# Low parts of the opening weights, and the decay of the recurrent states, moved between engines in a two-layer decoder kernel

## The chip, the cores and the metric

The kernel runs on one core of a Trainium2 chip. The metric is the time of one execution in microseconds of the device. The profile and the trace come from one execution on that core.

## What is computed

One step of a small decoder runs for 520 tokens at once: a prompt of 512 tokens and 8 sample tokens with caches of their own. Layer 0 is sliding-window attention beside a state-space scan, layer 1 is a gated DeltaNet; a SwiGLU feed-forward net, ffn(0) and ffn(1), follows each. Cut to what matters here:

```python
def swiglu(h, w_gate, w_up, w_down):
    return (jax.nn.silu(h @ w_gate) * (h @ w_up)) @ w_down

# gated_delta_rule, one step of the scan; a sample token is one such step
u = u0_c - jnp.einsum('bhik,bhkv->bhiv', kcd_c, s)
s = s * gl_c[..., None, None] + jnp.einsum('bhjk,bhjv->bhkv', kdec_c, u)

# trunk, per layer
h = rmsnorm(x, norm_mix_pre[l])
m = ...                                  # the mixer: projections of h, then the scan
x = x + rmsnorm(m, norm_mix_post[l])
f = swiglu(rmsnorm(x, norm_ffn_pre[l]), w_ffn_gate[l], w_ffn_up[l], w_ffn_down[l])
x = x + rmsnorm(f, norm_ffn_post[l])
```

The model width is 1024, the hidden width of the feed-forward net 2816. In layer 1, 16 heads for each of 8 sample tokens have a state of 128 x 128 that is read, multiplied by a decay, added to and written back.

## The kernel before

**Matmuls.** Activations lie with features on the partitions and tokens along the row, in two halves: half 0 has 256 tokens, half 1 has 264. Weights and activations are split into a high part that TensorE takes and the rest, the low part. Each product is the sum of three matmuls: high weight by high activation, high weight by low activation, low weight by high activation (`lin`). In the profile `whi` and `wlo` are the two parts of a weight block, and `Hh`, `Hl`, `p`, `bm` and `X` hold the two parts of activations in different stages.

**Weights.** A raw load (`raw`, two buffers, issued by SyncE's queue) brings 256 columns, two tiles of 128. `split` works on a unit of 128 x 512, half a tile's weights: it writes the high part, on ScalarE or, for each `hi_v`-th unit, on VectorE, and the low part, raw minus high, at line 193: on GpSimd for each `lo_pool`-th unit and on VectorE otherwise; `lo_pool` 0 means VectorE always. There are four buffers each for `whi` and `wlo`. The stages set both numbers: in layer 1's projections every low part goes to GpSimd, in ffn(1) every third.

**Parked low parts.** While ffn(0) runs, `park` loads 40 units of later weights (staged in `cs`), computes their low parts ahead of time (staged in `b`) and writes them to DRAM tensors named `pk`. When `split` meets such a unit it makes only the high part and loads the low part by a DMA on SyncE's queue. `PTILES` lists the tiles: of layer 1's first projection tiles 10 to 15, 0 to 7 and 16 to 21, in which 16 to 21 are the first six of the sixteen value tiles.

**Openings.** A stage's projection can begin when the norm of the stage before is done, first for half 0, then for half 1. So `group` does the first three or four tiles for half 0 and then for half 1: in ffn(0) and ffn(1) two gate tiles and two up tiles, in layer 1 a small tile of 32 columns and tiles 8 and 9. Their weights are prepared during the out projection of the stage before; the last tiles take buffers of their own (`p`, `b`, `cs`), since the ring has four. `out_proj` ends with `lo_pool` set to 1, so the units of the next opening group have their low parts on GpSimd, at the time at which VectorE does the norm (`rs`, `R`, then the products with `R`, the sums into the residual, and `Hl`).

**Layer 1's middle.** After the key and query tiles VectorE does the triangular elimination (line 302, `p` and `b`, with transposes at lines 1502, 1530 and 1531), while TensorE goes on with the value tiles; each is evacuated by VectorE (`cs<-acc,R`), and its convolution is shared by VectorE (`cs<-cs,cw`), ScalarE and GpSimd (`cs<-cs,p`, `cs<-cs,ex`).

**States.** `state_steps` runs in ffn(1): 34 steps, of which the inner 32 do a state block of one sample token and four heads. Step n stores block n-2, decays block n-1 (on GpSimd, `cs<-cs,small`, 128 x 512) and adds to it twice (VectorE, `cs<-b,CS,cs`, 128 x 256), and loads block n and its addend (`b<-ud`). ffn(1) goes through its 22 gate and 22 up tiles in 11 pairs of two and two, and takes a step after each tile from the second pair on, 40 places in all. The Silu of the gate tiles and the high casts of the hidden tiles are on ScalarE.

**Order.** The program is built by a scheduler that simulates the engines and orders each engine's instructions from it; the order in the source is only its input, marks such as `issue_after` and `high_priority` steer it. A changed instruction can therefore move others all over the program. Every engine, and every queue of DMAs, takes its instructions in the order emitted.

Of the kernel before, what the change touches and what calls it, by code (L numbers as in the profile page):

```python
# [13 lines left out]
ALU = mybir.AluOpType  # L14
# [104 lines left out]
 'yd': 'G'}  # L119


PTILES = [*range(10, 16), *range(8), *range(16, 22)]


def KN(n, v, *others):
# [97 lines left out]
class Ker:  # L223
# [112 lines left out]
    def group(s, w, xh, xl, nkt):  # L336

        w = [list(v) for v in w]
        ps = [{} for _ in w]
        for t in range(len(w)):  # L340
            if t % 2 == 0:
                a = s.acc()
            ps[t][0] = a[:, 256 * (t % 2):256 * (t % 2) + 256]
        for t in range(len(w)):
            ps[t][1] = (s.acc() if t < 2 else s.mx())[:, 0:HW[1]]
        for h in (0, 1):
            for t, v in enumerate(w):
                s.lin(v, xh, xl, nkt, (h,), ps[t])
        return ps

    def lnexp(s, ins):
# [145 lines left out]
    def out_proj(s, rows, xh, xl, nkt, mp, n, l, pre, tail=2, final=False):  # L497

        s.mp, s.sqs = mp, ([], [])
        if not final:  # L500
            tail = KN("tail%d%d" % (n, l), tail, 2, 3, 4)

        def evac(ps, ot):
            ins = None
            with s.tc.high_priority():
                for h in ps:
                    if ot == 7:
                        s.sqs[h].append(s.tms(HW[h]))
                        ins = s.act(s.sqs[h][0], ps[h], AF.Square)
                    if ot == 7 and final and h:  # L510
                        s.ts(mp[:, ot, HALF[h]], ps[h], s.gain(n, l, ot))
                    else:
                        s.act(mp[:, ot, HALF[h]], ps[h], scale=s.gain(n, l, ot))
                    if ot < 7:
                        s.add_sq(h, ps[h], ot == 0, s.tmp)
            return ins

        for ot in range(8 - tail):
            evac(s.lin(rows(ot), xh, xl, nkt), ot)
            if final and ot == 2:  # L520
                s.final_early()
        s.lo_pool = KN("lp_t%d%d" % (n, l), 2, 1, 3, 4)
        for h in (0, 1):
            for ot in range(8 - tail, 8):
                ins = evac(s.lin(rows(ot), xh, xl, nkt, (h,)), ot)
            if h == 0:
                with s.tc.issue_after(ins):
                    s.nc.scalar.preload_act_table_set("natural_log_exp_and_others")
                if final:
                    s.final_first()  # L530
                else:
                    s.pre = pre()
                    s.prenorm(*s.pre, 0, s.residual(n == 3, 0))
        if final:
            s.final_last()
        s.lo_pool, s.hi_v = 1, 0

    def spill(s):
        s.xd = s.dr.tile([128, KD * NT], F32, tag="xd", name="xd", bufs=2)
# [547 lines left out]
    def ffn(s, l):  # L1087
# [4 lines left out]
        x = s.lay("Hh"), s.lay("Hl")  # L1092
# [17 lines left out]
        if l == 0:  # L1110
            w = s.i["w_gdn_in"][0]
            s.copy_every = 0
            s.W.todo = [(w, 128 * t, k0) for t in PTILES for k0 in (0, 4)]
        s.lo_pool = KN("lp_f%d" % l, 1, 2, 3)
        s.hi_v = KN("hv_f%d" % l, 0, 2, 3, 4, 1)
        if l:
# [4 lines left out]
        for p in range(11):  # L1121
            sg = {}
            for t in (2 * p, 2 * p + 1):
                ps = first[t] if p == 0 else s.lin(s.W.tile(g, 128 * t, kts), *x, 8, ps=spare(t < 2 + KN("ma_f%d" % l, 0, 1, 2)))
                for h in (0, 1):
                    sl = (s.B("cs", NT * (t % 2), NT) if l == 0 else sgs if t % 2 else s.accT)[:, HALF[h]]
                    gt = s.tmp(HW[h])
                    with s.tc.high_priority():
                        s.tt(gt, ps[h], s.R2[:, HALF[h]], ALU.mult)
                    with s.tc.issue_after(s.norm_ins):  # L1130
                        ins = s.act(sl, gt, AF.Silu)
                    sg[t, h] = sl
                if l == 0 and p:
                    s.W.park(ins)
                if l and p:
                    next(states, None)
            for t in (2 * p, 2 * p + 1):
                ps = first[2 + t] if 2 + t < len(first) else s.lin(s.W.tile(u, 128 * t, kts), *x, 8)
                for h in (0, 1):
                    gt = s.tmp(HW[h])  # L1140
                    with s.tc.high_priority():
                        s.tt(gt, sg[t, h], ps[h], ALU.mult)
                    a = hh(t, h)
                    ins = s.act(a, gt)
                    s.tt(hl(t, h), gt, a.bitcast(F32), ALU.subtract)
                if l == 0 and p:
                    s.W.park(ins)
                if l and p:
                    next(states, None)
        for _ in states if l else ():  # L1150
            pass
# [715 lines left out]
    def state_steps(s):  # L1867
# [4 lines left out]
        gb = s.small(8, 2, 16)  # L1872
# [5 lines left out]
        for n in range(4 * NS + 2):  # L1878
            with s.tc.issue_after(s.last_load):
                if n > 1:  # L1880
                    s.dma(state(o["sgs"], n - 2), S(n - 2))
                if 0 < n < 4 * NS + 1:
                    t, (b, h) = S(n - 1), at(n - 1)
                    s.tt(t, t, gb[:, b, 0, h].unsqueeze(2).to_broadcast([128, 4, 128]), ALU.mult, s.nc.gpsimd)
                    for j in range(2):
                        v = slice(2 * j, 2 * j + 2)
                        s.stt(t[:, v], ub(n - 1)[:, v], s.kqs[:, h.start // 2 + j, b, 0:1], t[:, v], ALU.mult, ALU.add)
# [53 lines left out]
```

## Time and profile before

| | us |
|---|---|
| median of 3 runs (1893.59 to 1896.18) | 1893.84 |
| the profiled execution | 1886.62 |
| its span, first to last instruction | 1884.8 |
| TensorE busy | 1744.3 |
| VectorE busy | 1160.9 |
| ScalarE busy | 769.3 |
| GpSimd busy | 890.8 |

The mean granted clock of TensorE is 0.966. In rows of the profile, PE is TensorE's matmul, PEld its weight load, DVE is VectorE, ACT ScalarE, POOL GpSimd and SP SyncE. A row of a group gives line, engine, operation, output and inputs, shapes and count; then busy time and the mean of one in ns; then the idle time of the engine ahead of it and who ended that. A row of the timeline gives start, duration, engine, line, operation, and in brackets the idle time just before with what ended it. A row of the chain gives start and duration of a piece.

### The profile page before, as it was taken

The numbers are of one execution on the slowest core, as the hardware profiler recorded it, in microseconds if no ns is written. First come the engines' busy times: TensorE is split into PE (matmuls) and PEld (weight loads), VectorE is DVE, ScalarE is ACT, GpSimd is POOL, SyncE is SP. The second block draws the span as 40 slices with busy tenths as digits, with TensorE's granted clock in tenths as the row PEclk, the third lists the DMA queues.
The fourth block names the chain that finished last, engine by engine and source line by source line (L and its number), as shares of the span: only waits on it lengthen the run. The fifth ranks groups of instructions, "written<-read, shape, count | busy, mean of one in ns | idle before, by whom it ended". The sixth has DMA issues, their size and how long they took to land.

```text
span 1884.8 us, 36666 instructions
## 1 busy us (share of the span) xinstructions
PE 1744.3 (93%) x14263; PEld 1656.7 (88%) x14263; DVE 1160.9 (62%) x2325; ACT 769.3 (41%) x1868; POOL 890.8 (47%) x793
## 2 busy tenths in 40 slices
PE   7889999898999999989977888989999999999996
PEld 6878777598999999978977887888998999999995
DVE  6898879539433331168799967788703866753025
ACT  5432235555433333346765655644435311111222
POOL 2565657234666663342342564544557333323452
PEclk9999999898999999999988999999999999999998
DMA  7336766354556553346753113246435588863554
GB/s 258 129 126 184 221 193 179 130 154 126 157 182 189 185 175 100 92 141 212 245 172 112 43 45 110 60 125 186 135 91 180 160 257 262 262 206 123 160 160 152
DMA packets 328784, 300.39 MB, mean 159 GB/s; under 512 B 14529, under 2 KB 299910, under 8 KB 327442
## 3 DMA queue, kind: packets, MB, share of 16 engines
q1 hardware_dynamic: 327958, 297.37, 50.7%
q8 instruction: 112, 1.84, 0.4%
q10 hardware_dynamic: 652, 0.68, 0.1%
q14 instruction: 62, 0.51, 0.1%
HBM read 261.98 MB, written 72.52 MB: 177 GB/s over the span
## 4 chain that ended last, share of the span: by engine, by line
PE 50%; DVE 18%; DMA 9%; ACT 4%; issue 4%; POOL 2%; SPq 1%; DVEq 0%; ACTq 0%; POOLq 0%
PE acc L296 43%; PE ma L296 4%; DVE p L302 3%; DVE cs L309 3%; PE mb L296 2%; DMA b<-ud 2%; DMA raw<-in_w_ffn_down_dram 1%; DVE wlo L193 1%; ACT L312 1%; DMA cs<-in_state_gdn_dram 1%; POOL cs L302 1%; SPq L324 1%; DVE b L302 1%; DVE Hl L309 1%; PE mb L299 1%
## 5 line engine op out<-in xcount | busy, mean ns | idle before, releaser
L193 POOL TENSOR_TENSOR wlo<-raw,whi 128x512 fp32r<-128x512 f32 (+2 forms) x342 | 453.2, 1328 | 504.9 <-ACT whi L317 304.3
L296 PE MATMUL acc<-Hl,whi 128*128 128x256 f32 (+1 forms) x2576 | 561.4, 291 | 29.7 <-DVE cs L302 18.1
L296 PEld LDWEIGHTS acc<-Hl,whi 128*128 128x128 f32 x2576 | 419.2, 193 | 43.8 <-issue 18.8
L317 ACT CAST whi<-raw 128x512 fp32r<-128x512 f32 (+3 forms) x392 | 234.3, 603 | 436.2 <-PE acc L296 335.5
L296 PE MATMUL acc<-Hh,whi 128*128 128x256 f32 (+1 forms) x1824 | 390.2, 289 | 9.6 <-DVE sq L302 6.3
L296 PE MATMUL acc<-Hh,wlo 128*128 128x256 f32 (+1 forms) x1824 | 389.7, 289 | 1.2 <-DVE wlo L193 1.2
L296 PEld LDWEIGHTS acc<-Hh,whi 128*128 128x128 f32 x1824 | 293.6, 192 | 17.2 <-DVE sq L302 9.2
L296 PEld LDWEIGHTS acc<-Hh,wlo 128*128 128x128 f32 x1824 | 293.4, 192 | 9.0 <-issue 6.7
L296 PE MATMUL acc<-bm,whi 128*128 128x256 f32 (+1 forms) x1136 | 234.8, 290 | 0.1
L296 PE MATMUL acc<-p,whi 128*128 128x264 f32 (+1 forms) x1280 | 226.4, 284 | 0.0
L193 DVE TENSOR_TENSOR wlo<-raw,whi 128x512 fp32r<-128x512 f32 (+1 forms) x141 | 117.6, 835 | 140.3 <-ACT whi L317 137.7
L296 PEld LDWEIGHTS acc<-p,whi 128*128 128x128 f32 x1280 | 187.8, 190 | 0.8 <-DVE p L302 0.5
L296 PEld LDWEIGHTS acc<-bm,whi 128*128 128x128 f32 x1136 | 181.1, 193 | 2.8 <-issue 2.1
L318 DVE CAST whi<-raw 128x512 fp32r<-128x512 f32 x131 | 65.4, 503 | 179.8 <-PE acc L296 136.4
L296 PE MATMUL acc<-Hl,wlo 128*128 128x256 f32 (+1 forms) x752 | 169.7, 295 | 1.2 <-DMA wlo<-pk 0.7
L296 PE MATMUL acc<-p,wlo 128*128 128x256 f32 (+1 forms) x704 | 162.0, 284 | 7.1 <-DVE wlo L193 7.1
L296 PEld LDWEIGHTS acc<-Hl,wlo 128*128 128x128 f32 x752 | 126.1, 196 | 3.9 <-issue 1.6
L296 PEld LDWEIGHTS acc<-p,wlo 128*128 128x128 f32 x704 | 117.4, 189 | 8.0 <-DVE wlo L193 7.9
L296 PE MATMUL acc<-X,whi 128*128 128x264 f32 (+1 forms) x512 | 99.1, 288 | 1.1 <-ACT X L312 1.1
L309 DVE SCALAR_TENSOR_TENSOR cs<-cs,cw 128x512 f32<-128x512 f32 x100 | 90.4, 905 | 12.0 <-POOL cs L302 7.0
L302 POOL TENSOR_TENSOR cs<-cs,small 128x512 f32<-128x512 f32 x48 | 55.1, 1152 | 87.8 <-DMA cs<-in_state_gdn_dram 68.8
L296 PEld LDWEIGHTS acc<-X,whi 128*128 128x128 f32 x512 | 79.3, 193 | 2.4 <-ACT X L312 2.2
(466 smaller groups left out, 2989.6 us busy)
## 6 DMA issues: line engine op xcount, KB each, us to landing
raw<-in_w_gdn_in_dram SPq DMA_DIRECT2D x24, 1024.0 KB
raw<-in_w_ffn_gate_dram SPq DMA_DIRECT2D x22, 1024.0 KB
raw<-in_w_ffn_up_dram SPq DMA_DIRECT2D x22, 1024.0 KB
raw<-in_w_ffn_down_dram SPq DMA_DIRECT2D x20, 1024.0 KB
raw<-in_w_hyb_in_dram SPq DMA_DIRECT2D x16, 1024.0 KB
out_sv_dram<-in_cache_attn_v_dram SPq DMA_DIRECT2D x16, 1023.0 KB
out_sk_dram<-in_cache_attn_k_dram SPq DMA_DIRECT2D x16, 1023.0 KB
cs<-in_w_gdn_in_dram SPq DMA_DIRECT2D x40, 256.0 KB
```

The source lines that it names most:

```text
L193: eng.tensor_tensor(out=lo[:, :nk, d:d + n], in0=raw[:, :, o:o + n], in1=hi[:, :nk, d:d + n].bitcast(F32), op=ALU.subtract)
L296: s.nc.tensor.matmul(out, lhsT=lhsT, rhs=rhs, start=start, stop=stop, skip_group_check=skip)
L299: s.nc.tensor.transpose(out, in_, s.ident[0:in_.shape[0], 0:in_.shape[0]])
L302: return (eng or s.nc.vector).tensor_tensor(out=out, in0=a, in1=b, op=op).ins
L309: return s.nc.vector.scalar_tensor_tensor(out=out, in0=a, scalar=sc, in1=b, op0=op0, op1=op1).ins
L312: return s.nc.scalar.activation(out=out, in_=in_, func=f, **kw).ins
L317: return s.nc.scalar.copy(out, in_).ins
L318: return (s.nc.vector if e == "V" else s.nc.gpsimd).tensor_copy(out, in_).ins
L324: return (eng or s.nc.sync).dma_start(out=out, in_=in_).ins
```

## The change

Five edits:

1. The 40 parked units are others: tiles 8 and 9 of layer 1, the second and third of its opening group, come in, and the eight units of ffn(1)'s opening group; value tiles 16 to 21 go out.
2. `out_proj` ends with `lo_pool` 0 in place of 1: opening units that are not parked have their low parts on VectorE. In ffn(0) these are all eight, in layer 1 the two small ones of the 32-column tile.
3. In `group` the second half goes by row tiles, all tiles at one row tile and then the next.
4. The states begin one pair of tiles later, so 36 places are left for the 34 steps.
5. The decay of a state block is four activations of 128 x 128 with a scale per partition on ScalarE, in place of one multiplication of 128 x 512 on GpSimd.

```diff
-PTILES = [*range(10, 16), *range(8), *range(16, 22)]
+PTILES = [*range(8, 16), *range(8)]
...
-        for h in (0, 1):
+        for t, v in enumerate(w):
+            s.lin(v, xh, xl, nkt, (0,), ps[t])
+        for n in range(nkt):
             for t, v in enumerate(w):
-                s.lin(v, xh, xl, nkt, (h,), ps[t])
+                kt, hi, lo = v[n]
+                for lhs, x, st, sp in ((hi, xh, n == 0, False), (hi, xl, False, False), (lo, xh, False, n == nkt - 1)):
+                    s.mm(ps[t][1], lhs, x(kt, 1), st, sp)
...
-        s.lo_pool, s.hi_v = 1, 0
+        s.lo_pool, s.hi_v = 0, 0
...
-            s.W.todo = [(w, 128 * t, k0) for t in PTILES for k0 in (0, 4)]
+            s.W.todo = ([(w, 128 * t, k0) for t in PTILES for k0 in (0, 4)] +
+                        [(s.i[n][1], 128 * t, k0) for n in ("w_ffn_gate", "w_ffn_up") for t in (0, 1) for k0 in (0, 4)])
...
-                if l and p:
+                if l and p > 1:
                     next(states, None)
...
-                    s.tt(t, t, gb[:, b, 0, h].unsqueeze(2).to_broadcast([128, 4, 128]), ALU.mult, s.nc.gpsimd)
+                    for j in range(4):
+                        s.act(t[:, j], t[:, j], scale=gb[:, b, 0, h.start + j:h.start + j + 1])
```

GpSimd in layer 1's middle, before: `cs` are steps of the value tiles' convolutions, `X` and `p_9680` steps that prepare the elimination.

```order
L302 TENSOR_TENSOR cs<-cs,p_9678 128x512 x2
L551 MEMSET cs 128x3
L302 TENSOR_TENSOR cs<-cs,p_9678 128x512
L551 MEMSET cs 128x3 x2
L302 TENSOR_TENSOR p_9680<-cst,p_9680 128x1024
L302 TENSOR_TENSOR cs<-cs,p_9678 128x512
L302 TENSOR_TENSOR p_9680<-p_9680,small 128x1024
L302 TENSOR_TENSOR p_9680<-cst,p_9680 128x1024
L302 TENSOR_TENSOR cs<-cs,ex 128x512
```

And after, at the same place:

```order
L302 TENSOR_TENSOR cs<-cs,p_9678 128x512
L193 TENSOR_TENSOR wlo<-raw,whi 128x512
L302 TENSOR_TENSOR cs<-cs,p_9678 128x512
L193 TENSOR_TENSOR wlo<-raw,whi 128x512
L555 MEMSET cs 128x3
L193 TENSOR_TENSOR wlo<-raw,whi 128x512
L302 TENSOR_TENSOR cs<-cs,p_9678 128x512
L555 MEMSET cs 128x3
L193 TENSOR_TENSOR wlo<-raw,whi 128x512
L555 MEMSET cs 128x3
L302 TENSOR_TENSOR p_9680<-cst,p_9680 128x1024
L302 TENSOR_TENSOR cs<-cs,p_9678 128x512
```

The low parts of the value tiles now stand among these steps, where there was none.

GpSimd at the opening of ffn(0), as a difference: `acc` is a sum of squares, `ex` a step of the norm, and `wlo` and `p_5015` take the low parts of the opening group.

```order
 L302 TENSOR_TENSOR acc<-acc,sq 128x264
-L193 TENSOR_TENSOR wlo<-raw,whi 128x512 x4
-L193 TENSOR_TENSOR p_5015<-raw,p_5015 128x512 x4
 L306 TENSOR_SCALAR ex<-rs_4972 128x256
 L193 TENSOR_TENSOR wlo<-raw,whi 128x512 x4
```

Eight low parts leave GpSimd there. VectorE has them after, between the steps of half 0's norm:

```order
L302 TENSOR_TENSOR p_75<-p_75,p_74 128x256 x3
L309 SCALAR_TENSOR_TENSOR Hl<-p_75,par,Hh 128x256
L302 TENSOR_TENSOR p_74<-p_74,R_4695 128x256
L193 TENSOR_TENSOR wlo<-raw,whi 128x512
L309 SCALAR_TENSOR_TENSOR Hl<-p_75,par,Hh 128x256 x2
L302 TENSOR_TENSOR p_74<-p_74,R_4695 128x256
L302 TENSOR_TENSOR p_75<-p_75,p_74 128x256
L193 TENSOR_TENSOR wlo<-raw,whi 128x512
```

Before, the same piece of VectorE's order has the steps of the norm alone:

```order
L302 TENSOR_TENSOR p_75<-p_75,p_74 128x256 x3
L309 SCALAR_TENSOR_TENSOR Hl<-p_75,par,Hh 128x256
L302 TENSOR_TENSOR p_74<-p_74,R_4695 128x256
L309 SCALAR_TENSOR_TENSOR Hl<-p_75,par,Hh 128x256 x2
L302 TENSOR_TENSOR p_74<-p_74,R_4695 128x256
L302 TENSOR_TENSOR p_75<-p_75,p_74 128x256
L309 SCALAR_TENSOR_TENSOR Hl<-p_75,par,Hh 128x256
```

ScalarE in ffn(1) after: `acc` and `small` take the Silu of two gate tiles, `p_14391` the high parts of two hidden tiles, in two halves each, and `cs<-cs,small` are the decays.

```order
L312 ACTIVATE acc<-sq 128x256
L312 ACTIVATE acc<-sq 128x264
L312 ACTIVATE cs<-cs,small 128x128 x4
L312 ACTIVATE small<-sq 128x256
L312 ACTIVATE small<-sq 128x264
L312 ACTIVATE p_14391<-sq 128x256
L312 ACTIVATE p_14391<-sq 128x264
L312 ACTIVATE cs<-cs,small 128x128 x8
L312 ACTIVATE p_14391<-sq 128x256
L312 ACTIVATE p_14391<-sq 128x264
```

Before, ScalarE has the same rows here without the decays, which stand on GpSimd between low parts.

More of the change, by code (lines that the diff above doesn't have):

```diff
@@ L1147, in ffn @@
                     s.W.park(ins)
-                if l and p:
+                if l and p > 1:
                     next(states, None)
```

## The prediction

> **What bounds the kernel now.** I read first the page's busy times and the chain that ended last, then a table of stretches of time.
>
> ```profile
> PE 1744.3 (93%) x14263; PEld 1656.7 (88%) x14263; DVE 1160.9 (62%) x2325; ACT 769.3 (41%) x1868; POOL 890.8 (47%) x793
> PE 50%; DVE 18%; DMA 9%; ACT 4%; issue 4%; POOL 2%; SPq 1%; DVEq 0%; ACTq 0%; POOLq 0%
> ```
>
> TensorE is busy for 93% of the span, but it has only half of the chain: the stretches in which it waits are few, and there VectorE comes last. The change takes no matmul away, so all it can win is waiting, and the table says where that is (the third and fourth columns are PE and PEld, then DVE, ACT, POOL, and the granted clock):
>
> ```profile
> core 0: us, PE busy (x) PEld busy (x) DVE busy (x) ACT busy (x) POOL busy (x), PEclk, DMA share, GB/s
> 940.00:1060.00 120.00, 94.17 (x918) 91.85 (x918) 112.69 (x200) 73.90 (x216) 48.91 (x41) 0.87 0.41 132
> 1440.00:1460.00 20.00, 15.52 (x92) 13.57 (x91) 18.06 (x26) 11.08 (x24) 14.49 (x12) 0.80 0.58 200
> 1480.00:1500.00 20.00, 16.05 (x116) 15.52 (x116) 17.85 (x37) 5.84 (x13) 9.33 (x8) 0.91 0.74 237
> 1540.00:1680.00 140.00, 136.34 (x1109) 133.75 (x1108) 96.07 (x196) 18.34 (x48) 44.26 (x38) 1.00 0.78 253
> ```
>
> The opening of ffn(1), at 1440 to 1500 us, and layer 1's elimination, at 940 to 1060, run with VectorE 89 to 94% busy and TensorE waiting. At 1540 to 1680 (ffn(1)'s body, with the states) TensorE waits 3.7 of 140 us.
>
> **Part by part. A, the opening of ffn(1).** Half 0's norm on VectorE beside the low parts on GpSimd:
>
> ```profile
> 1445.59 1.46 POOL L193 TENSOR_TENSOR wlo<-raw,whi 128x512 fp32r<-128x512 f32 x1
> 1445.83 5.56 DVE L302 TENSOR_TENSOR p<-p,bm 128x256 f32<-128x256 f32 x5
> 1447.89 2.89 POOL L193 TENSOR_TENSOR wlo<-raw,whi 128x512 fp32r<-128x512 f32 x2
> 1451.84 0.39 PE L296 MATMUL acc<-Hl,whi 128*128 128x256 f32 x1 [2.33 <-DVE Hl L309]
> 1452.59 3.21 POOL L193 TENSOR_TENSOR wlo<-raw,whi 128x512 fp32r<-128x512 f32 x2 [1.81 <-ACT whi L317]
> 1453.18 1.49 DVE L309 SCALAR_TENSOR_TENSOR Hl<-p,par,Hh 128x256 fp32r<-128x256 f32 x1
> 1454.59 1.50 DVE L302 TENSOR_TENSOR bm<-bm,R 128x256 f32<-128x256 f32 x1
> 1456.35 0.47 DVE L309 SCALAR_TENSOR_TENSOR Hl<-p,par,Hh 128x256 fp32r<-128x256 f32 x1
> 1456.74 0.75 DVE L302 TENSOR_TENSOR p<-p,bm 128x256 f32<-128x256 f32 x2
> ```
>
> Two additions with GpSimd idle take 0.75 us together, five beside it 5.56; a Hl takes 0.47 alone and 1.49 beside a low part. A VectorE operation with two SBUF inputs is held up by about the GpSimd operation that it meets. The change loads these eight low parts from DRAM. The five additions then need 5 x 0.38 = 1.9 us: 3.6 us less. The Hl and the bm lose 1.0 us each, so half 0 is ready up to 5.6 us earlier (a little less, as GpSimd's sums of squares stay). TensorE waits 4.5 of these 20 us (20 - 15.52), and its clock of 0.80 says that 20 x 0.20 / 0.5 = 8 us ran at half: the waits, and 3.5 us of matmuls, which costs 1.7 more. Of this 6.2 I take 5.5, since the norm's own chain still ends near the end of the down projection. Ends: 3 (a low part comes late by DMA) and 8 (half 1's chain, contended too, also pays). **A = -5.5.**
>
> **B, the first states.** These stand on half 1's norm of the hidden layer's first tiles:
>
> ```profile
> 1485.97 3.42 POOL L302 TENSOR_TENSOR cs<-cs,small 128x512 f32<-128x512 f32 x3
> 1486.00 1.29 DVE L302 TENSOR_TENSOR rs<-rs,rs 128x264 f32<-128x264 f32 x1 [1.08 <-ACT rs L312]
> 1487.33 1.16 DVE L309 SCALAR_TENSOR_TENSOR rs<-rs,rs 128x264 f32<-128x264 f32 x1
> 1488.41 1.26 DVE L309 SCALAR_TENSOR_TENSOR cs<-b,CS,cs 128x256 f32<-128x256 f32 x1
> 1489.93 0.47 DVE L309 SCALAR_TENSOR_TENSOR cs<-b,CS,cs 128x256 f32<-128x256 f32 x1
> 1491.14 0.39 PE L296 MATMUL acc<-Hh,whi 128*128 128x256 f32 x1 [2.74 <-DVE sq L302]
> 1493.20 0.81 PE L296 MATMUL acc<-Hh,wlo 128*128 128x256 f32 x2 [1.22 <-DVE wlo L193]
> ```
>
> Three decays on GpSimd stretch the two rs steps, and updates of a state (cs) stand in front of the evacuation (sq) that frees the accumulator. One pair later, both are gone: (1.29 - 0.43) + (1.16 - 0.43) + 1.26 + 0.47 = 3.3 us less ahead of sq (the 0.43 is the same step undisturbed, row at 842.28 below). That takes the 2.74 and most of the 1.22, and with the clock at 0.91 (3.6 us at half, no more than the waits themselves here) little beside them. **B = -4**, ends -2.7 and -5.5. What is late next is the VectorE low part at 1493.20, 0.68 us long.
>
> **C, the states on ScalarE.** GpSimd's decays and the price on ScalarE of a like form:
>
> ```profile
> L302 POOL TENSOR_TENSOR cs<-cs,small 128x512 f32<-128x512 f32 x28 | 32.1, 1148 | 65.4 <-DMA cs<-in_state_gdn_dram 65.3
> L312 ACT ACTIVATE X<-X,small 128x128 f32<-128x128 f32 x32 | 10.0, 390 | 3.4 <-POOL X L302 3.4
> L296 PE MATMUL acc<-Hh,whi 128*128 128x256 f32 x185 | 52.4, 283 | 3.3 <-DVE sq L302 3.2
> ```
>
> A state costs 4 x 0.39 = 1.56 us on ScalarE in place of 1.15 on GpSimd, 50 us in all, on an engine with 18.34 of 140 us taken; that is covered. GpSimd no longer holds VectorE up, so part of TensorE's 3.3 us goes. But the DMA wait of 65.3 us in 22 cases (3 us each) moves from GpSimd, behind which only low parts stood, to ScalarE, behind which stand the Silu of the next pair and the casts of the hidden tiles. A Silu is used two tiles later: 1109 matmuls in 136.34 us are 0.123 us each, 48 to a tile, so some 11.8 us off, which covers 3 us. On SyncE's queue the states' loads and stores move a pair later with it, behind two more loads of weights; 36 slots are left for 34 steps, so they still end inside this stage. **C = -1.5**, ends -3.3 and +3 (one such wait that shows). [...]
>
> **D, the opening of layer 1.** Four low parts leave GpSimd:
>
> ```profile
> 842.28 0.43 DVE L302 TENSOR_TENSOR rs<-rs,rs 128x264 f32<-128x264 f32 x1 [0.95 <-ACT rs L312]
> 843.22 1.49 DVE L309 SCALAR_TENSOR_TENSOR R<-rs,rs 128x264 f32<-128x264 f32 x1
> 844.75 2.84 DVE L302 TENSOR_TENSOR Hh<-Hh,R 128x264 f32<-128x264 f32 x2
> 847.51 1.49 DVE L302 TENSOR_TENSOR p<-p,Hh 128x264 f32<-128x264 f32 x1
> 856.91 7.97 DMA wlo<-pk
> ```
>
> Four operations take 5.82 us where four at 0.43 would take 1.7: 4.1 us on the chain, as VectorE is all of it from 843 to 851. But later in the chain stands a low part's load of 7.97 us, and two more such loads (512 KB) now go ahead of it, 2 to 2.6 us at the 200 to 253 GB/s of the table's rows. **D = -2**, ends -4.5 and +2.
>
> **E, the opening of ffn(0).** Eight low parts move from GpSimd to VectorE:
>
> ```profile
> 435.85 2.90 DVE L309 SCALAR_TENSOR_TENSOR Hl<-p,par,Hh 128x256 fp32r<-128x256 f32 x2
> 438.67 1.50 DVE L302 TENSOR_TENSOR p<-p,R 128x256 f32<-128x256 f32 x1
> 442.68 4.08 DVE L309 SCALAR_TENSOR_TENSOR Hl<-p,par,Hh 128x256 fp32r<-128x256 f32 x3
> 446.68 1.51 DVE L302 TENSOR_TENSOR rs<-rs,rs 128x264 f32<-128x264 f32 x1
> 1492.46 0.68 DVE L193 TENSOR_TENSOR wlo<-raw,whi 128x512 fp32r<-128x512 f32 x1
> ```
>
> These seven take 9.99 us; alone, by the rows above, 5 x 0.47 + 2 x 0.43 = 3.2. So 6.8 us of stretch go, and 8 x 0.68 = 5.4 us of work come. **E = -1**, ends -2.5 and +2.
>
> **Second half by row tiles.** The order that the scheduler emits interleaves half 1 that way already, and half 1 has TensorE without a wait:
>
> ```profile
> 1464.00:1482.00 18.00, 18.00 (x150) 17.95 (x149) 18.00 (x47) 8.64 (x22) 3.22 (x3) 1.00 0.28 88
> ```
>
> So 0; were that cover gone, a wait like those of half 0 would come back, 1 to 2 us.
>
> **L, what pays for it.** The list of parked units keeps its length of 40, so tiles 16 to 21 lose their DRAM low parts: 12 units for GpSimd, in the elimination.
>
> ```profile
> L193 POOL TENSOR_TENSOR wlo<-raw,whi x8: 1257/1285/1718, 1007.8 to 1053.6; 128x512 fp32r<-128x512 f32 x8
> L296 PE MATMUL acc<-Hl,whi 128*128 128x256 f32 x95 | 29.7, 313 | 17.8 <-DVE cs L302 17.8
> L309 DVE SCALAR_TENSOR_TENSOR cs<-cs,cw 128x512 f32<-128x512 f32 x22 | 18.9, 860 | 1.3 <-POOL cs L302 1.2
> ```
>
> TensorE waits 17.8 us there for VectorE's evacuations, and VectorE has 112.69 of 120 us taken; what is added to it is added to the time. Twelve times 1.285 is 15.4 us of GpSimd work. [...] Half of 15.4, less a little idle time, is 7. Ends: +3 and +15.4. **L = +7.**
>
> **Sum:** -5.5 - 4 - 1.5 - 2 - 1 + 7 = -7.0 us on the profiled execution of 1886.62 us (its span is 1884.8). The runs shown have a median of 1893.84, 0.4% more; I put the difference on that: 1886.8.
>
> **Rivals.** *The elimination eats it (slower).* If a low part holds VectorE for its whole 1.285 us every time, L is +15.4, and the other terms at their weak side (-3, -2.7, 0, -1, 0 = -6.7) leave +8.7: 1902. For it: VectorE at 94%, and the pairs in A. Against: transposes and PSUM reads lie between. It decides from 1.2 us per low part on, where 12 of them pass the 14 us that the other terms bring as I take them. [...]
>
> *ScalarE stands behind the states (slower).* Where a wait and the Silus behind it pass the 11.8 us of slack, the up tiles wait. If 3 us come on the path in four of the nine pairs, C is +12 and the sum -5.5 - 4 + 12 - 2 - 1 + 7 = +6.5: 1900. For it: 22 of 28 decays found their state not yet loaded. Against: the slack, and ScalarE's 18 of 140 us.
>
> *Nothing in sum (same).* The waits of A and D are taken over by low parts that land late, as at 856.91 (A -3, D 0), B is -2.7, C and E are -1 together, and L is +7: about 0, 1894.
>
> [...]
>
> **How the numbers follow.** A measurement here tells apart about 0.2%, 3.8 us. Forecast (-4 to -12) 0.46, more 0.13, nothing in sum 0.18, elimination 0.15, ScalarE 0.08. Faster 0.59, same 0.18, slower 0.23. The range leaves out half of the elimination case and the far end of the gain: 1873 to 1900. The forecast's own range is 1882 to 1890.
>
> **What would show it.** Right: VectorE's additions at 1445 near 0.38 us each; no decay on GpSimd before 1505; the first evacuation of ffn(1)'s half 1 without the 2.74 wait; the stretch from layer 1's first v tile to its combine longer by 5 to 9 us. Wrong: that stretch no longer, or by over 13; waits of TensorE for wlo<-pk in the openings; a wait of ffn(1)'s up tiles for ScalarE.

## The result, and the profile after

The changed kernel takes 1869.06 us in the median of 4 runs (1863.11 to 1874.74) against 1894.27 us for the kernel before on the same chips: a ratio of 0.9865, with a 95% interval of 0.9827 to 0.9903. It is faster by 25 us, where 7 were forecast and 1873 was the lower end of the range. Run again beside other kernels it had a ratio of 0.9881 (0.9866 to 0.9896), 22.5 us. The profiled execution of it took 1865.10 us, with a span of 1863.3.

The table of stretches answers to the one of before; each window is moved to about where the same work stands now (8 us earlier in layer 1, 7 to 8 in ffn(1)'s opening, 18 in its body). Columns as before: PE, PEld, DVE, ACT, POOL, then the granted clock.

```profile
932.00:1052.00 120.00, 81.45 (x779) 79.03 (x777) 112.16 (x181) 66.56 (x192) 62.68 (x49) 0.86 0.25 82
1433.00:1453.00 20.00, 17.05 (x129) 15.64 (x128) 17.19 (x36) 13.93 (x33) 7.04 (x7) 1.00 0.94 327
1472.00:1492.00 20.00, 19.72 (x163) 19.35 (x162) 15.01 (x36) 8.68 (x23) 3.25 (x3) 1.00 0.66 217
1522.00:1662.00 140.00, 139.07 (x1148) 138.04 (x1147) 84.90 (x194) 47.05 (x141) 20.69 (x16) 1.00 0.83 271
```

Three of the four stretches have what was forecast or better. In ffn(1)'s opening TensorE waits 3.0 us in place of 4.5, and its clock is 1.00 in place of 0.80. From 1472 on it hardly waits, and in the body it waits 0.9 of 140 us in place of 3.7. The elimination got worse: TensorE is busy for 81 us of 120 in place of 94.

To see where each microsecond went, I took from each trace the starts of TensorE's matmuls, counted the same amount of matmul work in each, and noted the time from one mark to the next. The work is the same in all kernels of this table, so a smaller number is less waiting. All times in us, of one execution each; the profiled execution of the kernel before was shorter than its median, so before and after differ by 21.5 us of span here and not by 25:

```
                                  opening  opening  elimi-   com-   opening  first    body of  layer 0
                                  ffn(0)   layer 1  nation   bine   ffn(1)   states   ffn(1)
before                             56.5     73.4     94.3    163.6   45.9     46.6     172.6    407.6
group by row tiles alone           56.4     71.8     95.2    171.8   46.1     46.4     175.7    403.7
after                              52.8     66.8    106.3    154.6   40.4     41.2     168.7    404.1
after, second execution            54.0     66.3    107.6    152.9   40.4     41.2     168.4    404.0
after, values parked too           52.9     65.0     95.0    163.6   40.3     41.2     169.5    406.7
before, values not parked          56.4     73.2    106.9    165.5   46.3     46.7     175.9    409.2
before, tiles 8, 9 parked, v. not  56.6     67.3    109.7    154.7   45.8     48.7     175.5    409.1
after, decay on GpSimd             54.2     66.1    106.2    156.3   40.4     41.2     174.8    405.2
after, states a pair earlier       52.8     66.9    106.1    156.5   40.5     45.8     167.9    410.2
after, idle work on GpSimd         52.7     67.1    106.3    154.5   40.3     41.2     167.5    406.5
after, tiles 20, 21 parked too     54.7     65.0    108.0    154.3   40.5     40.8     167.7    406.2
```

Layer 0 shows how much one execution differs from another: 404 to 410 us with no pattern. Of the edits only the order by row tiles touches it; eight kernels without that edit, whose matmuls of layer 0 come in one and the same order, take 404 to 410 us there all the same. The openings repeat within a microsecond or two, and there the columns split cleanly by edit. The gain is in five columns, the loss in one, and the combine (the stage behind the elimination) moved by 9 to 11 us, which no step of the forecast had.

In ffn(1)'s opening, VectorE after:

```profile
1438.53 1.46 POOL L193 TENSOR_TENSOR wlo<-raw,whi 128x512 fp32r<-128x512 f32 x1
1438.77 3.39 DVE L302 TENSOR_TENSOR p<-p,bm 128x256 f32<-128x256 f32 x5
1443.94 0.47 DVE L309 SCALAR_TENSOR_TENSOR Hl<-p,par,Hh 128x256 fp32r<-128x256 f32 x1
1444.34 0.41 DVE L302 TENSOR_TENSOR bm<-bm,R 128x256 f32<-128x256 f32 x1
1442.61 0.39 PE L296 MATMUL acc<-Hl,whi 128*128 128x256 f32 x1 [0.15 <-DVE Hl L309]
```

The Hl that took 1.49 takes 0.47, the bm 0.41 for 1.50, and the wait of 2.33 for the first Hl has become 0.15; the later ones are waited for by 0.53 at most. The five additions take 3.39 and not 1.9, since one low part of the down projection still meets them.

### The profile page after: what moved, and what is told of

The parts are those of the page before. It is cut to its first block, busy times and chain, and to the rows that moved or that the text cites. A ratio compares the mean times of both kernels' runs of the same rounds, so it can differ in the third digit from the quotient of the medians.

```text
span 1863.3 us, 36784 instructions
## 1 busy us (share of the span) xinstructions
PE 1732.8 (93%) x14263; PEld 1649.8 (89%) x14263; DVE 1138.1 (61%) x2335; ACT 811.5 (44%) x1996; POOL 840.4 (45%) x751
## 5 line engine op out<-in xcount | busy, mean ns | idle before, releaser
L193 POOL TENSOR_TENSOR wlo<-raw,whi 128x512 fp32r<-128x512 f32 (+1 forms) x342 | 452.8, 1327 | 606.5 <-ACT whi L317 334.4
L296 PEld LDWEIGHTS acc<-Hl,whi 128*128 128x128 f32 x2576 | 415.6, 191 | 31.1 <-issue 11.4
L296 PE MATMUL acc<-Hh,whi 128*128 128x256 f32 (+1 forms) x1824 | 385.9, 286 | 7.2 <-DVE cs L302 3.4
L309 DVE SCALAR_TENSOR_TENSOR cs<-cs,cw 128x512 f32<-128x512 f32 x100 | 95.5, 956 | 13.9 <-POOL cs L302 9.7
L312 ACT ACTIVATE cs<-cs,small 128x128 f32<-128x128 f32 x128 | 41.1, 392 | 75.1 <-DMA cs<-in_state_gdn_dram 75.0
```

The source lines that it names most:

```text
L193: eng.tensor_tensor(out=lo[:, :nk, d:d + n], in0=raw[:, :, o:o + n], in1=hi[:, :nk, d:d + n].bitcast(F32), op=ALU.subtract)
L296: s.nc.tensor.matmul(out, lhsT=lhsT, rhs=rhs, start=start, stop=stop, skip_group_check=skip)
L309: return s.nc.vector.scalar_tensor_tensor(out=out, in0=a, scalar=sc, in1=b, op0=op0, op1=op1).ins
L312: return s.nc.scalar.activation(out=out, in_=in_, func=f, **kw).ins
```

## The experiments

The ratios below are to the kernel before, measured on the same chip beside it; in microseconds they are 1893 times the difference from one. The expectations were written with the trace after at hand. What they call the contention theory is the prediction's own account, that low parts on GpSimd hold VectorE up, with sizes by stage that were read from that trace.

**Each edit alone, on the kernel before.** First the list of parked units:

```diff
-PTILES = [*range(10, 16), *range(8), *range(16, 22)]
+PTILES = [*range(8, 16), *range(8)]
...
+                        [(s.i[n][1], 128 * t, k0) for n in ("w_ffn_gate", "w_ffn_up") for t in (0, 1) for k0 in (0, 4)])
```

> The kernel before with the other list of parked units alone. Contention theory, with the sizes that the trace after shows by stage: ffn(1)'s opening -5.4, layer 1's opening -6.4, the elimination +4 to +6.6, so -5 to -8 us. Forecast's sizes: -5.5 - 2 + 7 = -0.5. Rival (the gain lies in the new order that the scheduler makes all over the program): no fixed sign, and shifts of over 2 us in layer 0, where no edit does anything.

Measured: 0.9954 (0.9937 to 0.9972), 8.7 us faster. That is near the contention theory's size and not the forecast's, but the parts agree only in the openings. By equal work this kernel gains 6 us each in layer 1's and ffn(1)'s opening; its elimination costs 13 us, where 4 to 6.6 were expected, and its combine gains 10, which nobody expected. That the sum came out is in part luck.

```diff
-        s.lo_pool, s.hi_v = 1, 0
+        s.lo_pool, s.hi_v = 0, 0
```

> The kernel before with the opening low parts on VectorE in place of GpSimd alone, in all three openings (8, 6 and 8 units, none of them parked). Contention theory: ffn(0)'s opening -3.8 as in the trace after; in layer 1 and ffn(1) the stretch of VectorE's steps goes (4 and 5.6 us) and 0.68 us a unit comes (2.7 and 5.4), -1 each: -4 to -6 us. Forecast's sizes: -1 for ffn(0), about -3 in all. Rival (new order): layer 0 moves by over 2 us.

Measured: 0.9972 (0.9954 to 0.999), 5.3 us faster. In these three openings, in which VectorE is the engine waited for, low parts on VectorE beat low parts on GpSimd: by equal work ffn(0)'s and layer 1's opening gain 3.6 and 5.3 us, ffn(1)'s 1.0.

```diff
-        for h in (0, 1):
+        for t, v in enumerate(w):
+            s.lin(v, xh, xl, nkt, (0,), ps[t])
+        for n in range(nkt):
```

> The kernel before with the second half of the opening group by row tiles alone: no work is changed. Contention theory and forecast: 0, within 1 us. Rival (new order): 2 us or more either way, part of it in layer 0.

Measured: 0.9998 (0.9979 to 1.0018). Nothing, as forecast. Its layer 0 moved by 3.9 us in the profiled execution all the same. The edit does reorder a group there, but an unchanged layer 0 differs by over 5 us between traces as well, so a shift of that size says nothing of an edit, and the rival's sign in layer 0 is worthless.

```diff
-                if l and p:
+                if l and p > 1:
...
-                    s.tt(t, t, gb[:, b, 0, h].unsqueeze(2).to_broadcast([128, 4, 128]), ALU.mult, s.nc.gpsimd)
+                    for j in range(4):
+                        s.act(t[:, j], t[:, j], scale=gb[:, b, 0, h.start + j:h.start + j + 1])
```

> The kernel before with the states' decay on ScalarE and one pair later alone. Contention theory by the trace after: 1480 to 1500 us -5.4, the body of ffn(1) -4: -9 us. Forecast's sizes: -4 - 1.5 = -5.5. Rival (new order): less than 4, or layer 0 moves too.

Measured: 0.9963 (0.9943 to 0.9982), 7.0 us faster, between the two. By equal work the first states gain 5.2 us and the body 2.1. The four add up to 21 us; the whole change measured 22.5 to 25.

**Terms by themselves.** The changed kernel again, unchanged, beside the next three:

> The changed kernel again, to have its size beside the next three on one chip. If the edits add up (-8.7, -5.3, 0 and -7.0 alone): -21 us, ratio 0.989. If part of the first result was the run: less.

Measured: 0.9881 (0.9866 to 0.9896), 22.5 us. It adds up.

The price of the value tiles, by giving them back their parked low parts in the changed kernel, and by taking these away in the kernel before:

```diff
-PTILES = [*range(8, 16), *range(8)]
+PTILES = [*range(8, 16), *range(8), *range(16, 22)]
```

> The changed kernel with value tiles 16 to 21 parked as well, 52 units in all, the last 12 of them at the end of ffn(0)'s gate and up tiles. Contention theory (low parts on GpSimd hold VectorE in the elimination): faster than the changed kernel by L, 4 to 7 us, less 1 or 2 us for the further parking. Rival (the elimination does not pay, the low parts there meet transposes and idle): the same within 2 us, or slower.

Measured: 0.9858 (0.9844 to 0.9871), 4.4 us faster than the changed kernel on the same chip (medians 1865.31 and 1869.79). This is the fastest kernel of the study.

```diff
-PTILES = [*range(10, 16), *range(8), *range(16, 22)]
+PTILES = [*range(10, 16), *range(8)]
```

> The kernel before with value tiles 16 to 21 no longer parked and nothing in their place, 28 units: the price L by itself. Forecast: +7 (between +3 and +15.4). Rival (no price): 0 within 2 us.

Measured: 1.0076 (1.0061 to 1.0091), 14.4 us slower. Alone the term is twice what was forecast, near its far end; within the change it is 4.4. The difference is taken up below.

```diff
+            s.W.todo = ([(w, 128 * t, k0) for t in PTILES for k0 in (0, 4)] +
+                        [(s.i[n][1], 128 * t, k0) for n in ("w_ffn_gate", "w_ffn_up") for t in (0, 1) for k0 in (0, 4)])
```

> The kernel before with the eight units of ffn(1)'s opening parked as well, 48 units: the gain A by itself. Forecast: -5.5 (between -3 and -8). Rival (the low parts land late, or the next wait takes over): -1 to -2.

Measured: 0.9972 (0.9957 to 0.9987), 5.3 us faster. A was right.

```diff
-PTILES = [*range(10, 16), *range(8), *range(16, 22)]
+PTILES = [*range(8, 16), *range(8), *range(16, 22)]
```

> The kernel before with tiles 8 and 9 of layer 1's opening parked as well, 44 units: the gain D by itself. Forecast: -2 (between -4.5 and +2), since the loads of tile 10's low parts were to come later. Contention theory with the sizes of the trace after, where that wait is gone: -4 to -6.

Measured: 0.9974 (0.9954 to 0.9994), 4.9 us faster; D was forecast as 2.

**One edit undone, on the changed kernel.** These three were measured on another chip than the changed kernel itself, so their distance from it (0.9881) is good to some 4 us.

```diff
-        s.lo_pool, s.hi_v = 0, 0
+        s.lo_pool, s.hi_v = 1, 0
```

> The changed kernel with the unparked opening low parts back on GpSimd: eight in ffn(0), two small ones in layer 1. Forecast: 1 us slower than the changed kernel. By the trace after: 3.8 us slower. Rival (the gain of this edit came from layer 1 or ffn(1), where it had no parking beside it): the same.

Measured: 0.99 (0.9883 to 0.9916), 3.6 us slower than the changed kernel. The table puts it where it belongs: with the edit undone ffn(0)'s opening takes 56.4 us, as before.

```diff
-                    for j in range(4):
-                        s.act(t[:, j], t[:, j], scale=gb[:, b, 0, h.start + j:h.start + j + 1])
+                    s.tt(t, t, gb[:, b, 0, h].unsqueeze(2).to_broadcast([128, 4, 128]), ALU.mult, s.nc.gpsimd)
```

> The changed kernel with the states' decay back on GpSimd, still one pair later. Forecast: 1.5 us slower than the changed kernel (the body), B kept. By the trace after: 4 us slower. Rival (ScalarE behind the states costs): faster.

Measured: 0.9925 (0.9908 to 0.9942), 8.3 us slower; 6 of them are in the body's column (174.8 for 168.6), which differs by some microseconds between kernels of the same body too (see C below). The first states' column stays at 41.2.

```diff
-                if l and p > 1:
+                if l and p:
```

> The changed kernel with the states starting a pair earlier again, decay on ScalarE. If B came from GpSimd's decays alone, the start makes no difference: 0. If it came from VectorE's updates ahead of the evacuation as well (1.26 and 0.47 us of the 3.3): 1 to 2 us slower.

Measured: 0.9906 (0.9888 to 0.9925), 4.7 us slower, all of it in the first states' column (45.8 for 41.2). With the line above this says whose gain B is: not GpSimd's decays (they may stay on GpSimd, if late, and the column is 41.2), but the updates on VectorE in front of the evacuation. In the kernel that starts early TensorE waits for just that evacuation (sq), 3.47 us:

```profile
1488.20 0.58 PE L296 MATMUL acc<-Hh,whi 128*128 128x256 f32 x1 [3.47 <-DVE sq L302]
```

**What was still open: the elimination and the body.** The kernel before with both tiles 8 and 9 parked and the value tiles not:

```diff
-PTILES = [*range(10, 16), *range(8), *range(16, 22)]
+PTILES = [*range(8, 16), *range(8)]
```

> The kernel before with tiles 8 and 9 parked and value tiles 16 to 21 not, 32 units. If the parts add up as they were measured alone (-4.9 and +14.4): +9.5 us. If the low parts' price in the elimination stays (+12 there) but the order that the scheduler makes of the combine comes with this pair of edits (10 to 11 us less there, as in all five kernels that have both): about -3 us.

Measured: 0.999 (0.9977 to 1.0004), 1.9 us faster. The second expectation: the elimination's column is 109.7 and the combine's 154.7.

```diff
                     next(states, None)
+                    s.tt(s.tms(HN), sg[t, 1], s.cst[:, 0:HN], ALU.subtract, s.nc.gpsimd)
...
                     next(states, None)
+                    s.tt(s.tms(HN), a.bitcast(F32), s.cst[:, 0:HN], ALU.subtract, s.nc.gpsimd)
```

> The changed kernel with 36 extra subtractions of 128 x 264 on GpSimd in ffn(1)'s body, one after each tile, from data that is there in time; nothing uses what they give. They are as much GpSimd work with two SBUF inputs as the decays were (some 31 us), without the wait for the states' loads. If contention with VectorE made the decay on GpSimd dear: 4 to 5 us slower than the changed kernel. If GpSimd's queue standing behind the states' loads did: the same within 1 us.

Measured: 0.9887 (0.9864 to 0.991), 1.1 us slower than the changed kernel by ratios from two chips, within what they can tell; the body's column is 167.5. The wait of TensorE's weight loads, the first row of these two for the body of the kernel with the idle work and of that with the decay on GpSimd:

```profile
L296 PEld LDWEIGHTS acc<-Hh,whi 128*128 128x128 f32 x385 | 59.8, 188 | 1.4 <-DVE sq L302 1.3
```

```profile
L296 PEld LDWEIGHTS acc<-Hh,whi 128*128 128x128 f32 x368 | 58.0, 190 | 5.1 <-DVE sq L302 5.0
```

As much two-input work on GpSimd, but from data that is there: 1.4 us of waiting. The same with the wait for the states in front: 5.1. In the same two stretches VectorE, third in a row of stretches, is busy for as long in both, against 84.90 us in the changed kernel:

```profile
1523.00:1663.00 140.00, 139.27 (x1154) 138.55 (x1153) 94.89 (x199) 46.62 (x140) 47.10 (x40) 1.00 0.82 267
```

```profile
1532.00:1672.00 140.00, 136.79 (x1107) 134.88 (x1106) 94.60 (x192) 17.43 (x46) 44.09 (x37) 0.99 0.81 261
```

So VectorE was held up as much beside the idle work, and that cost nothing: contention as such did not make the decay on GpSimd dear. One part of it stays open. The states' updates, which come right behind the decays, take 0.67 us each with the decay on GpSimd and 0.53 with the idle work.

```diff
-PTILES = [*range(8, 16), *range(8)]
+PTILES = [*range(8, 16), *range(8), *range(20, 22)]
```

> The changed kernel with value tiles 20 and 21 parked as well, 44 units, which leaves eight of the twelve low parts in the elimination. The order of the combine stays as in the changed kernel. If the price goes by the number of low parts: 4 us faster than the changed kernel. If the first ones alone make it: the same.

Measured: 0.989 (0.9871 to 0.991), not faster than the changed kernel (1.7 us slower, from another chip); the elimination's column is 108.0. The price does not go by the number: the low parts of the first four value tiles are enough for all of it.

## Why the prediction was wrong, step by step

The sign was right, and the cause of most of the gain. Of the seven terms, A, B and the second half by row tiles came out as worked; C, D, E and L did not, and all four errors point the same way: 6.8 (or 4.4 by the stage alone), 2.9, 2.6 and 2.6 us. Together with 0.7 of B that is 15.6 us, the distance between the 7.0 of the sum and the 22.5 measured. That it comes out so well is luck: each of these sizes is good to some 4 us, and B and C, which measured 4.7 and 8.3 undone one by one, measured 7.0 together on the kernel before. What is clear of that is told by the columns of single stages, and by them the sum failed most in two places: layer 1's opening gained 6.6 us and not 2 (D), and the elimination with the combine behind it cost 3 and not 7 (L).

**A, -5.5: right, with a step that was not.** Alone it measured -5.3, and the changed kernel's column says -5.5. The clock is 1.00 after and 0.80 before, but I had it wrong which time ran at half. Before, it was granted like this:

```profile
1446.00:1452.10 6.10, 2.54 (x19) 2.12 (x19) 6.10 (x7) 3.04 (x7) 4.78 (x4) 1.00 0.55 172
1452.20:1462.30 10.10, 9.18 (x36) 7.65 (x35) 8.10 (x15) 6.94 (x17) 6.83 (x5) 0.50 0.58 208
```

The waits of 1.23 and 2.33 us lie in the first of these, at full speed, and half speed began behind them. So most of the 8 us at half were matmuls, some 7 and not 3.5, and by the sum's own rule they cost about 3.5 us and not 1.7. That the term came out all the same is in part luck.

**B, -4: right in size, half right in cause.** Undone it costs 4.7. The working had 1.6 us for two steps stretched by GpSimd's decays and 1.7 for the updates ahead of the evacuation. With the decay on ScalarE and the early start, these two steps are not stretched, and the column is no better. What costs is the queue: VectorE waited 2.60 us at an update of a state, and the norm's rs steps stood behind it. The kernel that starts early shows it:

```profile
1482.43 1.07 DVE L309 SCALAR_TENSOR_TENSOR cs<-b,CS,cs 128x256 f32<-128x256 f32 x2 [2.60 <-ACT cs L312]
1483.42 0.43 DVE L302 TENSOR_TENSOR rs<-rs,rs 128x264 f32<-128x264 f32 x1
1483.88 0.43 DVE L309 SCALAR_TENSOR_TENSOR rs<-rs,rs 128x264 f32<-128x264 f32 x1
```

Both rs steps take 0.43, undisturbed; the 2.60 us in front of them are the wait.

**C, -1.5: too small; the step that failed is its reach.** How much too small is known roughly. The body's column is 170 to 177 us in the nine kernels with the decay on GpSimd and 168 to 171 in the eight traces with it on ScalarE, some 5 us apart in the mean; the states' edit on the kernel before gained 2 there, and undoing it in the changed kernel cost 6. I took the 3.3 us from the row of TensorE's matmuls as all there was to win. The rows of the weight loads in the same stretch, before and then after, say otherwise:

```profile
L296 PEld LDWEIGHTS acc<-Hh,whi 128*128 128x128 f32 x370 | 57.8, 188 | 6.2 <-DVE sq L302 6.2
```

```profile
L296 PEld LDWEIGHTS acc<-Hh,whi 128*128 128x128 f32 x382 | 59.4, 188 | 2.0 <-DVE sq L302 1.7
```

A matmul row counts its modelled end of 0.28 us as busy (a mean of 283 ns in the prediction's row) where the next matmul would start after 0.12 (136.34 us for 1109 of them); each wait loses the difference in it. The weight load, which ends sooner (188 ns), shows 6.2 us before and 2.0 after, a gain of 4.2, of the size of the columns. The step's cause is in doubt as well: "GpSimd no longer holds VectorE up". The idle work on GpSimd speaks against it for this stage, in which VectorE has 84.90 of 140 us taken and so time to be held up in. What is left, and more argued than shown, is the order of waits in GpSimd's queue. VectorE's waits for decays, ahead of its evacuations, before and then after:

```profile
DVE cs L309 <- POOL cs L302: 22.3, 8, 4.9
```

```profile
DVE cs L309 <- ACT cs L312: 32.6, 21, 5.3
```

In sum they are no shorter after, but they come in pieces of 1.6 us, not of 2.8, so an evacuation behind one of them is held less long. On GpSimd, from 1540 to 1680 us in the kernel before, a decay stood behind low parts, 17 of them with 44.0 us of waiting, 33.8 of it for a high cast on VectorE, and these behind decays, 21 with 51.4 us of waiting for a load. Which of the two waits matters was not tried. The feared wait on ScalarE is there in full, and nothing comes of it:

```profile
L312 ACT ACTIVATE cs<-cs,small 128x128 f32<-128x128 f32 x105 | 33.7, 392 | 68.0 <-DMA cs<-in_state_gdn_dram 67.9
```

A state costs 4 x 0.392 us as forecast, and the 68 us of waiting move to ScalarE as forecast; the slack of two tiles covers them. So the rival of ScalarE behind the states falls.

**D, -2: the term that failed is the +2 for loads that come later.** The chain of VectorE shortened as worked (4.1). But the low parts' loads do not push each other back. SyncE's queue before and after:

```profile
836.88 0.58 SPq L324 DMA_DIRECT2D out_sk_dram<-in_cache_attn_k_dram  x1
839.92 9.18 SPq L324 DMA_DIRECT2D raw<-in_w_gdn_in_dram  x2
856.52 0.34 SPq L324 DMA_DIRECT2D xd<-p  x1
856.91 4.83 SPq L324 DMA_DIRECT2D wlo<-pk  x4
```

```profile
829.51 1.05 SPq L324 DMA_DIRECT2D wlo<-pk  x2
830.60 0.67 SPq L324 DMA_DIRECT2D out_sk_dram<-in_cache_attn_k_dram  x1
846.69 0.81 SPq L324 DMA_DIRECT2D wlo<-pk  x2
```

Before, tile 10's low parts were asked for at 856.91, behind a copy of a megabyte, two raw loads and a spill, and landed 8 us later, TensorE waiting for the last 1.1 us. After, the opening's low parts go ahead of that copy, and the next two are asked for at 846.69 and not 856.91, since the buffers that they need come free sooner. No matmul of this opening waits for a low part's load any more. The step counted the bytes of the loads, and not the time at which each is issued. The time of the whole program with this edit alone, -4.9 us with an interval from -1 to -9, would not tell it from the -2; the opening does, which by equal work takes 6 us less in that run.

**E, -1: the step that failed is that it left the clock out.** The VectorE part was right: the eight low parts take 0.68 us and less, and the norm's steps are back at 0.4.

```profile
433.26 0.68 DVE L193 TENSOR_TENSOR wlo<-raw,whi 128x512 fp32r<-128x512 f32 x1
433.86 0.87 DVE L309 SCALAR_TENSOR_TENSOR Hl<-p,par,Hh 128x256 fp32r<-128x256 f32 x2
438.20 1.89 DVE L193 TENSOR_TENSOR p<-raw,p 128x512 fp32r<-128x512 f32 x3
```

The same 34 us of the opening, before and then after:

```profile
420.00:454.00 34.00, 28.17 (x192) 26.27 (x192) 29.84 (x51) 20.98 (x48) 16.59 (x13) 0.85 0.63 194
```

```profile
413.00:447.00 34.00, 30.72 (x224) 28.91 (x224) 27.93 (x60) 23.33 (x52) 7.40 (x7) 0.95 0.71 217
```

Waiting fell from 5.8 to 3.3 us, and the clock rose from 0.85 to 0.95. The part of this time at half speed, before and then after:

```profile
438.40:448.60 10.20, 7.17 (x28) 6.13 (x29) 10.13 (x15) 5.46 (x13) 7.02 (x6) 0.50 0.54 154
```

```profile
437.80:441.10 3.30, 3.10 (x13) 2.98 (x14) 3.30 (x9) 1.70 (x6) 0.00 (x0) 0.50 0.95 303
```

Of matmuls, 7.17 us ran at half before and 3.10 after. At 0.50 a matmul takes 0.26 us in the first of these rows (7.17 for 28) and 0.24 in the second (3.10 for 13); at 1.00, in ffn(1)'s body before, it takes 0.12 (136.34 for 1109). Taking half of each for the clock, I estimate its cost at 3.6 us before and 1.6 after. That is 2.5 us of waiting and 2.0 of clock, somewhat more than the column's -2.5 to -3.7. In A I had counted the clock; in E I had not.

**L, +7: the elimination costs 12, and 10 of it come back in the next stage.** That VectorE bounds the elimination and that GpSimd's work is added to it is right; the share was too small. That it would be half was my estimate, and no run shows it. What the traces show is that a low part holds up some of VectorE's steps and not others. In the kernel after, an evacuation of two halves (`cs<-acc,R`) takes 0.75 us beside a low part at 973.52 and 0.75 without one at 958.04; the eight transposes at line 1502 of the kernel before take 1.91 to 2.06 us each, those beside a low part among them. The convolution's step of 128x512 takes 1.79 at 956.33 beside a low part and 0.74 without one at 958.92. And a cast of 128x512, which reads one input, takes 1.23 us at 1546.62 in the kernel before, beside a low part, and 0.42 at 1545.61 without one. Over the same matmuls, before and then after:

```profile
954.30:1048.50 94.20, 71.09 (x642) 69.24 (x642) 88.64 (x169) 57.03 (x165) 40.65 (x32) 0.86 0.36 114
```

```profile
941.50:1047.80 106.30, 70.53 (x644) 68.41 (x644) 100.07 (x167) 58.70 (x166) 57.17 (x44) 0.84 0.22 74
```

GpSimd is busy for 16.5 us more, and VectorE, with no more instructions, for 11.4; I had taken half of 15.4. TensorE waits 12.7 us more. Here is one place in the kernel after, GpSimd, VectorE and TensorE:

```profile
970.57 2.79 POOL L302 TENSOR_TENSOR p<-cst,p 128x1024 f32<-128x1024 f32 x1
973.32 1.41 POOL L193 TENSOR_TENSOR wlo<-raw,whi 128x512 fp32r<-128x512 f32 x1
974.69 2.34 POOL L302 TENSOR_TENSOR p<-cst,p 128x1024 f32<-128x1024 f32 x1
976.99 1.71 POOL L193 TENSOR_TENSOR wlo<-raw,whi 128x512 fp32r<-128x512 f32 x1
```

```profile
971.08 2.52 DVE L302 TENSOR_TENSOR b<-p 128x220 f32<-128x220 f32 x1
974.67 2.90 DVE L309 SCALAR_TENSOR_TENSOR cs<-cs,cw 128x512 f32<-128x512 f32 x1
977.50 1.44 DVE L302 TENSOR_TENSOR p<-p,b 128x220 f32<-128x220 f32 x1
980.95 1.25 DVE L302 TENSOR_TENSOR sd<-small 128x32 f32<-128x32 f32 x1
```

```profile
982.35 0.37 PE L299 MATMUL mb<-cst,sd 128*32 128x128 f32 x1 [14.48 <-DVE sd L302]
```

GpSimd works without a gap, and VectorE's steps on b, cs and p take 1.4 to 2.9 us beside it; with GpSimd idle, at 980.88 and 981.18 in the kernel before, the step on p takes 0.37 and that on cs 0.74. (The steps on p are on GpSimd before as well; the low parts between them are new.) A small VectorE step (sd) stands in order behind them; TensorE waits 14.48 us for it, with the value tiles' matmuls behind that wait. With the values parked the same matmul waits 5.50 us:

```profile
978.71 0.37 PE L299 MATMUL mb<-cst,sd 128*32 128x128 f32 x1 [5.50 <-DVE sd L302]
```

Eight low parts cost as much as twelve: there the wait is 13.43 us. But this one wait is not the whole price. In the kernel with the states' edit alone, whose value tiles are parked, it is 12.41 us, and the elimination takes some 96 us, since other waits there are shorter:

```profile
991.11 0.37 PE L299 MATMUL mb<-cst,sd 128*32 128x128 f32 x1 [12.41 <-DVE sd L302]
```

So the price is VectorE's longer time, and at which waits TensorE pays it differs with the order. Why eight low parts cost as much as twelve stays open. It was 1.0 us per low part by the column, under the 1.2 from which the rival of the elimination was to decide, but with the openings paying more than their middle it would not have decided there either.

What gives it back is the combine: 153 to 157 us in all eight kernels with tiles 8 and 9 parked and 16, 17, 18 and 19 not, 163 to 172 in the eight others, those that the table leaves out among them. TensorE's two largest waits there before were

```profile
1090.38 1.12 PE L299 MATMUL mb<-cst,ex 128*128 128x128 f32 x4 [5.49 <-DVE ex L309]
1144.67 0.95 PE L296 MATMUL ma<-p 128*128 128x128 f32 x4 [3.79 <-DVE Hh L302]
```

and after no wait for ex or Hh there is above 2 us; the longest is this:

```profile
1067.94 0.66 PE L299 MATMUL mb<-cst,ex 128*128 128x128 f32 x4 [1.94 <-DVE ex L309]
```

In all TensorE waits 20 us there before and 12 after. No instruction of the combine was changed; the scheduler wrote it in another order. The experiment with both edits on the kernel before (-1.9 us where the parts alone add up to +9.5) shows that this order comes with the pair of them. Neither half has it: with the values not parked alone the combine takes 165.5, with tiles 8 and 9 parked alone 163.4. That the order is the cause is inferred from this, and what in the order does it was not found; an order of the combine exchanged by itself was not tried, nor was a kernel with the values parked and this order, which would join the best columns of the table.

Of the outcomes beside the forecast, the larger gain ("more", 0.13) came nearest: the clock rose in the openings, from 0.80 to 1.00 in ffn(1)'s and from 0.85 to 0.95 in ffn(0)'s, and the elimination with the combine behind it cost 3 us and not 7, by another order of the combine. The rival that in sum nothing happens, with low parts landing late, is refuted by D's rows.

## What to carry to other kernels

Look at where an engine's wait stands in its queue and not only at how long its operations take: moving loads ahead of a large copy, moving updates that wait out of the way of an evacuation and, as far as the runs tell, moving a wait to a queue with slack behind it (the decay to ScalarE) won more than the operations cost. Read TensorE's waiting from the weight loads' rows as well as from the matmuls', and add the clock's part wherever the granted clock of a stretch is under 1. Where a scheduler writes the order, give each stage's time before and after by equal work, and expect stages that no edit touches to move by 10 us: a term measured alone (14.4) and in company (4.4) can differ by as much.

## What the runs showed of the hardware

- The clock fell behind a wait of 2.33 us. In ffn(1)'s opening before, TensorE waited 2.33 us, and matmuls of 128x256 took 0.41 us behind it in place of 0.28:

```profile
1449.23 0.28 PE L296 MATMUL acc<-p,wlo 128*128 128x264 f32 x1
1451.84 0.39 PE L296 MATMUL acc<-Hl,whi 128*128 128x256 f32 x1 [2.33 <-DVE Hl L309]
1453.73 0.41 PE L296 MATMUL acc<-Hh,whi 128*128 128x256 f32 x1
```

  The granted clock is 1.00 up to 1452.10 and 0.50 behind it (the rows under A). In the kernel after, with waits of 1.32 us and less, the clock of the stretch is 1.00. A wait of 2.33 us in one piece, with one of 1.23 us that had ended 1.6 us before it began, was enough here. Nor is 1.32 us a safe length: in ffn(0)'s opening after, the clock fell at 437.8 though no wait in the 4.0 us before was over 1.12 us. TensorE was busy for 2.17 of these 4.00 us; that it is the share of waiting that counts is my reading of this one place, and was not tried:

```profile
433.80:437.80 4.00, 2.17 (x10) 1.35 (x10) 4.00 (x10) 3.94 (x10) 0.00 (x0) 1.00 0.03 4
```
- GpSimd is held up as well as VectorE. In the kernel before, two sums of squares (`acc<-acc,sq`, 128x256 and 128x264) took 1.45 us together at 391.78, with VectorE idle, and one of 128x264 took 1.22 at 433.00, beside two additions and an Hl. A subtraction of 128x264 on GpSimd took 0.80 us in one group and 1.42 in another of the kernel with idle work:

```profile
L302 POOL TENSOR_TENSOR sd<-p,cst 128x264 f32<-128x264 f32 x8 | 11.3, 1419 | 23.5 <-DVE wlo L193 21.2 <-ACT p L312 2.3
L302 POOL TENSOR_TENSOR sd<-small,cst 128x264 f32<-128x264 f32 x6 | 4.8, 802 | 36.8 <-ACT small L312 36.8
```

  The price was in none of the columns of the kernel with idle work.
